# Output projection of a hybrid mLSTM and sparse-attention block: weight quarters through GpSimd's queue, T4 summed early in B22's place, four joins by copies and accumulating DMAs

## The chip, the core and the metric

The kernel runs on one core of a Trainium2 chip. A core has five engines with an instruction queue each: TensorE (PE, matrix products, with PEld for its weight loads), VectorE (DVE), ScalarE (ACT), GpSimd (POOL) and SyncE (SP). An engine runs its own queue in order, and waits on semaphores of the others. DMA transfers are issued from the queues of SP, ACT and POOL; only those issued by POOL may accumulate into what they write. Products land in PSUM, which has eight banks of 128 x 512 float32; everything else lies in SBUF. The metric is the device time of one execution in microseconds (us).

## What is computed

The reference is one decoder layer. Its last part is what matters here:

```
ya = sigmoid(p["m_o"]) * mh * silu(p["m_z"])          # 512 x 1024, branch A
yb = yn * silu(p["n_z"])                              # 512 x 512,  branch B
merged = (sigmoid(p["g_a"]) * (ya @ w_branch_a)
          + sigmoid(p["g_b"]) * (yb @ w_branch_b))    # 512 x 1024
x = x + merged @ w_out                                # 1024 x 1024 weight
return _rmsnorm(x, final_norm_g)
```

All of it is float32. The kernel gets that accuracy by splitting each operand into a rounded high part and the rest (`split`: ACT writes the high part, DVE the low one) and by three matmuls for each product: high by high, high by low, low by high.

## The kernel before

The change lies in the last 100 us, in the block at lines 1231 to 1422.

**Branch A** comes first: eight jobs, one for each block of 128 output columns, in the order j = 0, 4, 1, 5, 2, 6, 3, 7 (L1275). A job is 24 matmuls into one PSUM bank of the tag `pp`, which has three (`branch`, L1111). Its weights come by SP as a 512 KB tile `wr` (three places) and are split into `wh` and `wl` (four places each); its gate `s` (three places, 256 KB) comes by SP from HBM too. A job's loads and the split of its weights are traced two jobs ahead of its matmuls (`Stream`, L164). After the matmuls DVE forms `s = (s + 1) * ps` (L1121) and adds it to branch B's part (`merge`, L1267), which gives a finished block `merged[j]`; `settle` splits the block of the job before into `meh` and `mel`; and after j = 4, 5, 6 `merged_sums` forms the sums and differences that the next part needs, and splits them into `mSh` and `mSl`.

**The output projection** multiplies the 512 x 1024 matrix `merged` by W_out with seven block products in place of eight (Strassen's method in Winograd's form). Tokens and features of `merged` are halved, and W_out is cut into quarters B11, B12 (first 512 rows; left and right columns), B21, B22. Besides quarters, the products take four sums:

- T3 = B12 + B22, T2 = T3 + B11, T4 = T2 + B21, T1 = B12 + B11.

The products are, in TensorE's order, M11 (by B11), M12 (by B21), M22 (by T4), MS2 (by T2), MS3 (by T3), MS1 (by T1), MS4 (by B22); each is 24 matmuls for each of two token blocks, every one of which reads a 128-row block of merged features. M11 needs the blocks j = 0 to 3, so it ends up waiting for job 7 (j = 3) and M12 for job 8 (j = 7). Every factor is made by `hilo`, which splits two half-quarter tiles of 128 x 1024 with the same four `wh` and `wl` places as the branch weights.

How the factors come in before: SP loads B12 into a tile `T` and B22 into tiles `R`, and POOL adds B22 onto that copy by two accumulating DMAs (`added`, L1287), which gives T3. B11, B12 (a second time) and B21 come into `R` by SP. DVE forms T2 = T3 + B11 (L1302). POOL adds B11 onto the second B12, which gives T1. T4 = B21 + T2 is formed by DVE behind M11 (L1376), in B21's place. So W_out is read 1.25 times.

The results go to `xo`, which starts as the residual x. `aside` copies a PSUM bank by ACT, scaled by 0.5 or -0.5, and POOL adds the copy to `xo` by an accumulating DMA: M11 (L1374), and X after MS2 and MS3. `join` has DVE add a bank to `xo` itself (L1334); `joined` adds to that a square by ACT, for the norm, and DVE's product with the final norm's weight.

What sets the order: the functions are traced in the order of the text, but a planner may move every instruction that isn't held, by its own model of durations. `tc.keep_in_program_order` pins an instruction behind the one traced just before it on its engine. Here TensorE is held from L1312 on, and nothing of DVE, ACT, POOL and SP is, except one table load: `ordered` was cleared earlier. So the order of merges, sums, splits and transfers in the profile is the planner's. A place of a tile with several (`bufs`) is given on when its last reader is done.

Of the kernel before, what the change touches and what calls it, by code (L numbers as in the profile page):

```python
# [11 lines left out]
F32 = mybir.dt.float32  # L12
# [3 lines left out]
OP = mybir.AluOpType  # L16
AX = mybir.AxisListType.X

T = 512
D = 1024  # L20
NT = T // 128
ND = D // 128
# [10 lines left out]
NG, NZ, GA, GB = 6408, 6432, 6944, 7968  # L33
# [29 lines left out]
def build(  # L63
# [4 lines left out]
    nc = tc.nc  # L68
    ordered = {"act", "dve"}

    class Engine:
# [3 lines left out]
        def __getattr__(self, op):  # L75
# [7 lines left out]

            return call

    pe, pool = Engine(nc.tensor, "pe"), nc.gpsimd
    act, dve = Engine(nc.scalar, "act"), Engine(nc.vector, "dve")
    A = act.activation
# [40 lines left out]
    def split(src, hi, lo, eng="a"):  # L129
        if eng == "a":  # L130
            A(hi, src, AF.Copy)
        elif eng == "p":
            pool.tensor_scalar(hi, src, 1.0, 1.0, OP.mult, OP.mult)
        else:
            dve.tensor_copy(hi, src)
        dve.tensor_tensor(lo, src, f(hi), OP.subtract)
# [27 lines left out]
    class Stream:  # L164
# [3 lines left out]
        def add(self, load, gen):  # L168
            self.jobs.append((load, gen))
# [56 lines left out]
    stream = Stream(2)  # L226
# [13 lines left out]
    cs = pers.tile([128, NT, 4], F32, name="cs")  # L240
# [36 lines left out]
    def hilo(qs):  # L277
        out = []
        for q in qs:
            hi = wp.tile([128, 2, 512], F32R, name="wh", tag="wh", bufs=4)  # L280
            lo = wp.tile([128, 2, 512], F32R, name="wl", tag="wl", bufs=4)
            split(q, hi, lo)
            out.append((hi, lo))
        return out

    with tc.tile_pool(name="ph0", bufs=2, side="right") as p0, tc.tile_pool(
        name="small", bufs=1, side="right"
# [10 lines left out]
        for k in (0, 4):  # L298
            ks = slice(k, k + 4)
# [10 lines left out]
        for hf in range(2):  # L310
            ps = PS()
# [67 lines left out]
        for tb in range(NT):  # L379
            ts = slice(tb * 128, (tb + 1) * 128)  # L380
            for hf in range(2):
                ks = slice(hf * 4, hf * 4 + 4)
# [55 lines left out]
        split(b, *parts["S1"])  # L438
        split(d, *parts["S4"])

    def plus(dst, a, b):
        for d, x, y in zip(dst, a, b):
            dve.tensor_tensor(d, x, y, OP.add)
        return dst

    def product(banks, k, ws, start=True, tbs=(0, 1), cs=slice(0, 512)):
        ah, al = parts[k]
        for tb in tbs:
            ts = slice(tb * 128, tb * 128 + 128)
            for c in range(4):  # L450
                wh, wl = (w[:, c % 2, cs] for w in ws[c // 2])
                first, last = start and c == 0, c == 3
                m = lambda l, r, first=False, last=False: pe.matmul(
                    banks[tb][:, cs], l, r, start=first, stop=last, skip_group_check=True
                )
                m(ah[:, c, ts], wh, first)
                m(ah[:, c, ts], wl)
                m(al[:, c, ts], wh, False, last)
# [179 lines left out]
    load = lambda: next(more)  # L638
# [372 lines left out]
    late = deque()  # L1011
# [46 lines left out]
    yah = yap.tile([128, ND, T], F32R, name="yah", tag="yah")  # L1058
    yal = yap.tile([128, ND, T], F32R, name="yal", tag="yal")

    sgp = ctx.enter_context(tc.tile_pool(name="sgp", bufs=3))
# [40 lines left out]
    wov = w_out[0].rearrange("(k p) c -> p k c", p=128)  # L1102
# [3 lines left out]
    def branch(base, j, yh, yl, nk):  # L1106
        def gen(w):
            o = 0 if nk == ND else (j % 2) * 128
            ps = PP()
            yield from passes(  # L1110
                ps, lambda k: w[0][:, k, o : o + 128], lambda k: w[1][:, k, o : o + 128],  # L1111
                lambda k: yh[:, k], lambda k: yl[:, k], nk,
            )
            s = halves.pop((base, j))
            if base == GB:
                if not merged:
                    merged.append(pers.tile([128, ND, T], F32, name="mB", tag="hTh"))
                dve.scalar_tensor_tensor(merged[0][:, j], s, 1.0, ps, OP.add, OP.mult)
            else:
                dve.scalar_tensor_tensor(s, s, 1.0, ps, OP.add, OP.mult)  # L1120
                merge(j, s)  # L1121

        def load():
            halves[base, j] = sgp.tile([128, T], F32, name="s", tag="s")
            nc.sync.dma_start(halves[base, j], gD[base, j])
            if nk == ND:
                return weights(wav[:, :, j * 128 : j * 128 + 128])
            if j % 2 == 0:
                halves["w"] = weights(wbv[:, :, j * 128 : j * 128 + 256])
            return halves["w"]  # L1130

        stream.add(load, gen)
# [10 lines left out]
    for h in range(4):  # L1143
# [11 lines left out]
        for sb in range(NT):  # L1155
            o, n = KOFF[sb], 512 - sb * 128
# [6 lines left out]
        for sb in range(NT):  # L1163
            o, n = KOFF[sb], 512 - sb * 128
# [13 lines left out]
        for tb in range(NT):  # L1178
            po = PT()
            for sb in range(tb + 1):  # L1180
                a = KOFF[sb] + (tb - sb) * 128
# [49 lines left out]
    with tc.tile_pool(name="fin", bufs=1, reuse_waits="tile") as fp:  # L1231
# [10 lines left out]
        def merged_sums(i):  # L1242
            a, b = merged[0][:, i], merged[0][:, i + 4]
            a1, a2, b1, b2 = a[:, :256], a[:, 256:], b[:, :256], b[:, 256:]
            dve.tensor_tensor(b2, a2, b2, OP.subtract)
            dve.tensor_tensor(a2, a1, a2, OP.subtract)
            dve.tensor_tensor(a1, b2, a1, OP.subtract)
            dve.tensor_tensor(b1, a1, b1, OP.add)
            sums_split(i, a, 0)

        def sums_split(i, t, c):
            split(
                t, Sh_[:, i, c : c + 2, :].rearrange("p s t -> p (s t)"),
                Sl_[:, i, c : c + 2, :].rearrange("p s t -> p (s t)"),
            )
# [8 lines left out]

        def merge(j, s):
            m = merged[0][:, j]
            dve.tensor_tensor(m, s, m, OP.add)  # L1267
            waiting.append(j)
            if len(waiting) > 1:
                k = settle()  # L1270
                if k in (4, 5, 6):
                    merged_sums(k - 4)

        tc.keep_in_program_order(act.preload_act_table_set("natural_log_exp_and_others"))
        for j in (0, 4, 1, 5, 2, 6, 3, 7):  # L1275
            branch(GA, j, yah, yal, ND)

        def tiles(tag, bufs):
            return [fp.tile([128, 2, 512], F32, name=tag, tag=tag, bufs=bufs) for _ in range(2)]

        def load(i, j, ts):
            for n, t in enumerate(ts):
                ks = slice(i * 4 + n * 2, i * 4 + n * 2 + 2)
                nc.sync.dma_start(t, wov[:, ks, j * 512 : j * 512 + 512])
            return ts

        def added(ts, more):  # L1287
            for t, m in zip(ts, more):
                pool.dma_start(t, m, accum_op=OP.add)
            return ts  # L1290

        t3 = load(0, 1, tiles("T", 4))
        b22 = load(1, 1, tiles("R", 8))
        added(t3, b22)
        stream.run()
        b11 = load(0, 0, tiles("R", 8))
        stream.run()
        b12 = load(0, 1, tiles("R", 8))
        stream.run()
        b21 = load(1, 0, tiles("R", 8))  # L1300
        stream.run()
        t2 = plus(tiles("T", 4), t3, b11)  # L1302
        stream.run(2)
        t1 = added(b12, b11)
        w1 = hilo(b11)
        stream.run()
        settle()
# [6 lines left out]
        xo = yap.tile([128, NT, D], F32, name="xo", tag="yah")  # L1314
        for tb in range(NT):
            nc.sync.dma_start(xo[:, tb], x[0, tb * 128 : tb * 128 + 128, :])
        late = yap.tile([128, 8, 512], F32, name="late", tag="yal")
# [7 lines left out]

        def aside(banks, n, j, half, scale):
            for i, bank in enumerate(banks):
                t, tb = late[:, n * 2 + i], half * 2 + i
                A(t, bank, AF.Copy, scale=scale)
                pool.dma_start(xo[:, tb, j * 512 : j * 512 + 512], t, accum_op=OP.add)  # L1330

        def join(tb, cs, bank):
            xv = xo[:, tb, cs]
            dve.scalar_tensor_tensor(xv, bank, 0.5, xv, OP.mult, OP.add)  # L1334
            return xv

        def joined(tb, cs, bank, n):
            xv = join(tb, cs, bank)
            A(junk[:, tb * 2 + n % 2, : cs.stop - cs.start], xv, AF.Square, accum_out=fs[:, tb, n : n + 1])
            dve.tensor_tensor(xv, xv, fg[:, cs], OP.mult)  # L1340

# [5 lines left out]

        L, R = slice(0, 512), slice(512, 1024)

        def left(tb, bank):  # L1350
            joined(tb, L, bank, 0)
            part_sum(tb, 1)

# [19 lines left out]
        product(X, "M11", w1)  # L1373
        aside(X, 0, 0, 0, 0.5)  # L1374
        Z = [PP() for _ in range(2)]
        t4 = plus(b21, b21, t2)  # L1376
        w4 = hilo(t4)
        product(Z, "M12", w2)
        merged_sums(3)
        w6 = hilo(t2)  # L1380
        V = [PT() for _ in range(2)]
        product(V, "M22", w4)
        ordered.difference_update(("act", "dve"))
        for i in range(2):
            left(i, Z[i])
        for i in range(4):
            sums_split(i, merged[0][:, i + 4], 2)
        for i in range(2):
            join(2 + i, L, V[i])
        w7 = hilo(t3)  # L1390
        product(X, "MS2", w6, False)
        aside(X, 1, 1, 0, -0.5)
        w5 = hilo(t1)
# [51 lines left out]
```

## Time and profile before

| | us |
|---|---|
| median of three runs | 634.77 (634.74 to 635.29) |
| the profiled execution | 637.34 |
| its span, first to last instruction | 635.3 |
| PE busy in the span | 608.0 (96%) |
| DVE busy | 494.0 (78%) |
| ACT busy | 345.9 (54%) |
| POOL busy | 59.1 (9%) |

The profile shows one execution. The timeline lists instructions by start, duration, engine, line, operation, output and inputs, with the idle time of the engine just before them and what ended it in brackets. Nearly all compute instructions have line 79, that of a helper, so they are told apart by their tiles: `pp<-yah,wh` is branch A, `ps<-wh,meh` is M11, `mel<-mB,meh` is the low part of a finished block. Busy times of matmuls overlap: their starts, 0.23 us apart, are the pace. The table of windows gives busy time (and count) of each engine in a stretch, the granted clock of TensorE as a share of full speed, the busy share of the DMA engines, and GB/s.

### The profile page before, as it was taken

The numbers are of one execution on the slowest core, as the hardware profiler recorded it, in microseconds if no ns is written. First come the engines' busy times: TensorE is split into PE (matmuls) and PEld (weight loads), VectorE is DVE, ScalarE is ACT, GpSimd is POOL, SyncE is SP. The second block draws the span as 40 slices with busy tenths as digits, with TensorE's granted clock in tenths as the row PEclk, the third lists the DMA queues.
The fourth block names the chain that finished last, engine by engine and source line by source line (L and its number), as shares of the span: only waits on it lengthen the run. The fifth ranks groups of instructions, "written<-read, shape, count | busy, mean of one in ns | idle before, by whom it ended". The sixth has DMA issues, their size and how long they took to land.

```text
span 635.3 us, 8633 instructions
## 1 busy us (share of the span) xinstructions
PE 608.0 (96%) x3014; PEld 502.5 (79%) x3014; DVE 494.0 (78%) x962; ACT 345.9 (54%) x650; POOL 59.1 (9%) x124
## 2 busy tenths in 40 slices
PE   5999999999999999999999999999999999987995
PEld 3988878888888877888888788887878788866784
DVE  4799979596685777876868676989898986459966
ACT  5645457554442456665665665666565643125564
POOL 4000000000000001221312130000000000100120
PEclk9999999999999999999999999999999999999898
DMA  7925644502067442131322213513232337993324
GB/s 240 336 92 165 214 134 122 173 5 83 18 176 197 107 127 83 51 84 50 84 57 77 84 39 97 146 36 99 67 100 67 100 116 200 297 249 105 111 50 150
DMA packets 83643, 76.02 MB, mean 120 GB/s; under 512 B 4960, under 2 KB 64516, under 8 KB 83600
## 3 DMA queue, kind: packets, MB, share of 16 engines
q1 hardware_dynamic: 82016, 71.53, 37.5%
q0 software_dynamic: 1440, 3.67, 3.3%
q8 instruction: 24, 0.39, 0.3%
q10 hardware_dynamic: 144, 0.26, 0.1%
q14 instruction: 19, 0.16, 0.1%
HBM read 62.35 MB, written 8.39 MB: 111 GB/s over the span
## 4 chain that ended last, share of the span: by engine, by line
PE 67%; DVE 16%; DMA 5%; ACT 5%; issue 4%; POOL 1%; SPq 1%; POOLq 0%; ACTq 0%; DVEq 0%
PE pp L79 38%; PE ps L79 16%; PE pt L79 10%; PE po L79 3%; DVE u L79 3%; DVE wl L79 2%; ACT wh L79 2%; DMA T<-R 1%; DMA R<-w_out 1%; DVE mB L79 1%; DMA wr<-w_branch_a 1%; DVE Dm L79 1%; DMA xt<-x 1%; DVE Sl L79 1%; DVE Th L79 1%
## 5 line engine op out<-in xcount | busy, mean ns | idle before, releaser
L79 PE MATMUL pp<-hTh,wh 128*128 128x512 f32 (+1 forms) x360 | 142.6, 396 | 0.0
L79 PE MATMUL pp<-hTl,wh 128*128 128x512 f32 (+1 forms) x360 | 140.0, 389 | 0.0
L79 PE MATMUL pp<-hTh,wl 128*128 128x512 f32 (+1 forms) x360 | 139.8, 388 | 0.0
L79 ACT ACTIVATE wh<-wr 128x1024 fp32r<-128x1024 f32 x56 | 59.0, 1058 | 59.2 <-PE pp L79 43.9
L79 DVE TENSOR_TENSOR wl<-wr,wh 128x1024 fp32r<-128x1024 f32 x56 | 68.2, 1219 | 17.0 <-ACT wh L79 16.9
L79 PEld LDWEIGHTS pp<-hTh,wl 128*128 128x128 f32 x360 | 67.7, 188 | 13.1
L79 PEld LDWEIGHTS pp<-hTh,wh 128*128 128x128 f32 x360 | 67.8, 188 | 10.6
L79 PEld LDWEIGHTS pp<-hTl,wh 128*128 128x128 f32 x360 | 67.9, 189 | 9.9
L959 POOL TENSOR_SCALAR P<-P,st 128x128 f32<-128x128 f32 (+1 forms) x64 | 34.6, 560 | 160.9 <-DVE st L79 69.0
L79 DVE TENSOR_TENSOR wl<-R,wh 128x1024 fp32r<-128x1024 f32 x28 | 33.9, 1221 | 12.8 <-ACT wh L79 12.7
L79 DVE TENSOR_TENSOR wl<-T,wh 128x1024 fp32r<-128x1024 f32 x28 | 33.8, 1222 | 10.4 <-ACT wh L79 10.4
L79 ACT ACTIVATE P<-P,st 128x128 f32<-128x128 f32 (+3 forms) x64 | 35.5, 555 | 11.2 <-DVE st L79 10.7
L79 ACT ACTIVATE pth<-pt 128x512 fp32r<-128x512 f32 (+1 forms) x64 | 26.9, 434 | 25.9 <-PE pt L79 14.6
L79 DVE TENSOR_TENSOR ptl<-pt,pth 128x512 fp32r<-128x512 f32 (+1 forms) x64 | 29.9, 485 | 14.2 <-ACT pth L79 13.7
L79 DVE CUSTOM_DVE_ANT_0 P<-ps,cst 128x128 f32<-128x128 f32 (+3 forms) x64 | 30.5, 487 | 12.7 <-PE ps L79 12.5
L79 ACT ACTIVATE wh<-R 128x1024 fp32r<-128x1024 f32 x28 | 29.1, 1054 | 16.3 <-PE pt L79 7.1
L79 DVE SCALAR_TENSOR_TENSOR u<-pp,prm,u 128x511 f32<-128x511 f32 (+2 forms) x48 | 35.7, 744 | 0.2
L79 ACT ACTIVATE wh<-T 128x1024 fp32r<-128x1024 f32 x28 | 29.1, 1055 | 12.1 <-PE ps L79 5.6
L79 PE MATMUL ps<-k,Th 128*128 128x256 f32 (+2 forms) x112 | 29.1, 341 | 1.4 <-PE pp L79 0.8
L79 PE MATMUL pt<-cst,P 128*128 128x128 f32 x160 | 28.4, 277 | 0.9 <-DVE ptl L79 0.8
L79 PEld LDWEIGHTS pt<-cst,P 128*128 128x128 f32 x160 | 19.7, 140 | 10.9 <-DVE ptl L79 5.8
L79 PE MATMUL pp<-yah,wh 128*128 128x512 f32 x64 | 25.0, 391 | 2.1 <-ACT wh L79 2.1
(350 smaller groups left out, 1392.6 us busy)
## 6 DMA issues: line engine op xcount, KB each, us to landing
wr<-w_in SPq DMA_DIRECT2D x44, 512.0 KB, 4.0
R<-w_in SPq DMA_DIRECT2D x24, 512.0 KB, 4.6
gD<-sg SPq DMA_DIRECT2D x16, 256.0 KB, 2.0
s<-gD SPq DMA_DIRECT2D x16, 256.0 KB, 5.8
wr<-w_branch_a SPq DMA_DIRECT2D x8, 512.0 KB, 4.1
R<-w_out SPq DMA_DIRECT2D x8, 512.0 KB, 9.5
vD<-cq SPq DMA_DIRECT2D x8, 256.0 KB, 3.7
wr<-vD SPq DMA_DIRECT2D x4, 512.0 KB, 4.1
```

Source lines behind the costliest of these rows:

```text
L79: ins = fn(*args, **kw)
L959: pool.tensor_scalar(pj, pj, st[:, 2, j : j + 1], 1.0, OP.mult, OP.mult)
```

## The change

All four quarters of W_out are loaded by POOL's queue, held there ahead of the first branch A job, each once. T3 becomes a sum by DVE behind job 3, T2 one behind job 4, T4 one behind job 5, written into B22's place; B22 is loaded a second time by SP, behind the second product, for MS4. T1 is still made by POOL, now behind T2. The instructions of `branch` and `merge`, and the three sums, are held in program order on DVE. M12's and M22's two banks each are no longer joined by DVE: `aside` copies them by ACT into places of the tag `s` and POOL adds them to `xo`; `left` of the first two token blocks then starts from `xo`. The split of T3 (`w7`) is traced ahead of it.

```diff
+    keep = tc.keep_in_program_order
...
-    def plus(dst, a, b):
+    def plus(dst, a, b, held=lambda ins: ins):
         for d, x, y in zip(dst, a, b):
-            dve.tensor_tensor(d, x, y, OP.add)
+            held(dve.tensor_tensor(d, x, y, OP.add))
...
-                dve.scalar_tensor_tensor(s, s, 1.0, ps, OP.add, OP.mult)
+                keep(dve.scalar_tensor_tensor(s, s, 1.0, ps, OP.add, OP.mult))
                 merge(j, s)
...
-            dve.tensor_tensor(m, s, m, OP.add)
+            keep(dve.tensor_tensor(m, s, m, OP.add))
...
-        for j in (0, 4, 1, 5, 2, 6, 3, 7):
-            branch(GA, j, yah, yal, ND)
-
...
-        def load(i, j, ts):
+        def load(i, j, ts, queue=pool):
             for n, t in enumerate(ts):
                 ks = slice(i * 4 + n * 2, i * 4 + n * 2 + 2)
-                nc.sync.dma_start(t, wov[:, ks, j * 512 : j * 512 + 512])
+                keep(queue.dma_start(t, wov[:, ks, j * 512 : j * 512 + 512]))
...
-        t3 = load(0, 1, tiles("T", 4))
-        b22 = load(1, 1, tiles("R", 8))
-        added(t3, b22)
+        b12, b22, b11, b21 = (load(i, j, tiles("R", 8)) for i, j in ((0, 1), (1, 1), (0, 0), (1, 0)))
+        for j in (0, 4, 1, 5, 2, 6, 3, 7):
+            branch(GA, j, yah, yal, ND)
+
+        stream.run(3)
+        t3 = plus(tiles("T", 4), b12, b22, keep)
         stream.run()
-        b11 = load(0, 0, tiles("R", 8))
+        t2 = plus(tiles("T", 4), t3, b11, keep)
+        t1 = added(b12, b11)
         stream.run()
-        b12 = load(0, 1, tiles("R", 8))
+        t4 = plus(b22, t2, b21, keep)
         stream.run()
-        b21 = load(1, 0, tiles("R", 8))
-        stream.run()
-        t2 = plus(tiles("T", 4), t3, b11)
-        stream.run(2)
-        t1 = added(b12, b11)
         w1 = hilo(b11)
...
             for i, bank in enumerate(banks):
-                t, tb = late[:, n * 2 + i], half * 2 + i
+                t = sgp.tile([128, T], F32, name="s", tag="s") if n is None else late[:, n * 2 + i]
+                tb = half * 2 + i
...
-            xv = join(tb, cs, bank)
+            xv = xo[:, tb, cs] if bank is None else join(tb, cs, bank)
...
-        def left(tb, bank):
+        def left(tb, bank=None):
...
         Z = [PP() for _ in range(2)]
-        t4 = plus(b21, b21, t2)
         w4 = hilo(t4)
         product(Z, "M12", w2)
+        b22 = load(1, 1, tiles("R", 8), nc.sync)
         merged_sums(3)
         w6 = hilo(t2)
+        aside(Z, None, 0, 0, 0.5)
         V = [PT() for _ in range(2)]
         product(V, "M22", w4)
         ordered.difference_update(("act", "dve"))
-        for i in range(2):
-            left(i, Z[i])
         for i in range(4):
             sums_split(i, merged[0][:, i + 4], 2)
+        aside(V, None, 0, 1, 0.5)
+        w7 = hilo(t3)
         for i in range(2):
-            join(2 + i, L, V[i])
-        w7 = hilo(t3)
+            left(i)
```

## The prediction

> **What bounds the kernel now.** I read the page first: TensorE is busy for 96% of the span, so a gain must come from gaps or a low clock of TensorE, or from the tail behind its last matmul. Its waits from the start of branch A on name all the gaps there are:
>
> ```profile
> PE ps L79 <- ACT meh L79: 3.2, 1, 3.2
> PE pp L79 <- ACT wh L79: 2.1, 1, 2.1
> PE pp L79 <- DVE wl L79: 0.5, 1, 0.5
> ```
>
> The timeline of TensorE gives their places, and the table of windows the clock:
>
> ```profile
> 535.54 0.39 PE L79 MATMUL pp<-yah,wh 128*128 128x512 f32 x1
> 567.96 0.39 PE L79 MATMUL pp<-yah,wl 128*128 128x512 f32 x1
> 570.41 0.50 PE L79 MATMUL pp<-yah,wh 128*128 128x512 f32 x1 [2.07 <-ACT wh L79]
> 572.00 0.39 PE L79 MATMUL pp<-yah,wh 128*128 128x512 f32 x1
> 584.04 0.39 PE L79 MATMUL ps<-wh,mel 128*128 128x512 f32 x1
> 587.61 0.80 PE L79 MATMUL ps<-wh,meh 128*128 128x512 f32 x1 [3.18 <-ACT meh L79]
> 594.22 0.40 PE L79 MATMUL pp<-wh,meh 128*128 128x512 f32 x1
> 627.12 0.28 PE L79 MATMUL pp<-wh,mSl 128*128 128x256 f32 x1
> 585.00:588.00 3.00, 0.39 (x1) 0.39 (x2) 3.00 (x6) 1.91 (x3) 0.00 (x0) 0.86 0.96 362
> 588.00:594.00 6.00, 6.00 (x15) 4.26 (x15) 5.97 (x9) 2.58 (x4) 0.87 (x1) 0.50 0.45 183
> ```
>
> The 144 matmuls of jobs 1 to 6 start from 535.54 to 567.96: 0.2267 us each, 5.44 a job. Against that pace three things are lost. (a) Job 7: from 567.96 to 572.00 lie four steps, 4.04 us for 0.91: **3.13**. (b) M11's tenth matmul, the first that reads block j = 3: 3.57 for 0.23: **3.34**. (c) The 15 matmuls behind it ran at clock 0.50: 594.22 - 587.61 = 6.61 for 3.40: **3.21**. Together **9.68 us**. From 594.22 to the last matmul nothing is lost.
>
> Where do (a) and (b) come from? The timelines of DVE, SP and POOL, read backwards, meet in one wait:
>
> ```profile
> 541.18 0.69 DVE L79 SCALAR_TENSOR_TENSOR s<-s,pp 128x512 f32<-128x512 f32 x1 [3.35 <-PE pp L79]
> 543.65 0.69 DVE L79 TENSOR_TENSOR mel<-mB,meh 128x512 fp32r<-128x512 f32 x1
> 552.57 1.23 DVE L79 TENSOR_TENSOR T<-T,R 128x1024 f32<-128x1024 f32 x1 [8.23 <-DMA T<-R]
> 553.71 0.68 DVE L79 SCALAR_TENSOR_TENSOR s<-s,pp 128x512 f32<-128x512 f32 x1
> 587.95 0.69 DVE L79 TENSOR_TENSOR mel<-mB,meh 128x512 fp32r<-128x512 f32 x1
> 534.65 1.23 SPq L1284 DMA_DIRECT2D R<-w_out  x2
> 542.62 0.34 SPq L1125 DMA_DIRECT2D s<-gD  x1
> 556.15 0.34 SPq L1125 DMA_DIRECT2D s<-gD  x1
> 558.49 0.53 SPq L143 DMA_DIRECT2D wr<-w_branch_a  x1
> 543.88 1.08 POOL L1289 DMA_DIRECT2D T<-R  x1 [16.69 <-DVE wl L79]
> 569.30 1.06 ACT L79 ACTIVATE wh<-wr 128x1024 fp32r<-128x1024 f32 x1 [7.80 <-DMA wr<-w_branch_a]
> ```
>
> DVE's queue has T2 ahead of job 2's merge. T2 waits 8.23 us for T3, which goes from HBM to `R` (from 534.65) and then through an accumulating DMA (from 543.88). Job 2 was done at 535.54 + 2 x 5.44 = 546.4, but its merge begins at 553.71. SP's next gate load waits for that merge (556.15), and job 7's weights stand behind it: issued at 558.49, split at 569.30. That is (a). DVE, late by then, is busy without a gap to the end of M11, and block 3 is ready only with 587.95. That is (b), and (c) follows (b).
>
> **The change part by part.** *Loads and T3.* The copy of B12 (1 MB) and T3's accumulating DMA go; DVE gets T3: two sums of 128x1024 at 1.23 us, behind job 3. T2 can't block job 2 or 3 any more, as the holds put it behind job 4. SP loses ten issues between its gate loads, and job 7's weights wait only for the merge of job 2 or so, some 7 us earlier. I count (a) as gone.
>
> *Do the quarters land in time?* No row shows a plain load by POOL. The nearest rows:
>
> ```profile
> R<-w_out SPq DMA_DIRECT2D x8, 512.0 KB, 9.5
> T<-R POOLq DMA_DIRECT2D x2, 512.0 KB, 9.5
> s<-gD SPq DMA_DIRECT2D x7, 256.0 KB, 8.8
> 540.00:545.00 5.00, 5.00 (x24) 4.14 (x23) 3.12 (x4) 1.70 (x2) 1.08 (x1) 1.00 1.04 384
> 550.00:555.00 5.00, 5.00 (x23) 4.14 (x23) 2.43 (x3) 0.00 (x0) 0.42 (x1) 1.00 0.93 205
> 592.54 0.87 POOL L1330 DMA_DIRECT2D xo<-late  x1 [34.89 <-ACT late L79]
> 618.74 0.87 POOL L1330 DMA_DIRECT2D xo<-late  x1 [2.13 <-ACT late L79]
> ...
> wr<-w_branch_a SPq DMA_DIRECT2D x8, 512.0 KB, 4.1
> ```
>
> Eight issues of 0.87 us are 7 us of POOL. If they start where SP's did (534.65), 4.2 MB and 1.8 MB of gates and weights beside them need 16 to 29 us at 384 to 205 GB/s: all there by 550 to 564, and B12 with B22, the first half, by 543 to 550. T3 stands behind job 3 (551.9) and its sums, at about 556, T2 at about 561, T4 at about 569. At the worst pace a row allows, that of the accumulating pair (9.5 us for two half quarters), they land at 544, 554, 563 and 573; that end is the first rival. I take the upper ends of the plain rates, which are loads from the same tensor: no wait.
>
> The issues kept to 0.87 us where DVE was busy for 5.97 of 6.00 us (588 to 594), so DVE did not hold them up. The Trainium skill, "SBUF — State Buffer", section "SBUF: two separate sides", speaks against the move: while DVE runs an operation that takes the port it shares with GpSimd, GpSimd can't write the descriptors of its DMAs, and loads from SP or ACT don't suffer this. By that, were each of the eight issues held by one sum of 1.23 us, the last quarter would come 10 us later, at up to 574, T4 would wait 5 us, and the time would be the first rival's; the two rows show no hold.
>
> *T4 moved.* Two sums of 1.22 leave the stretch behind M11 and enter branch A, ahead of job 6's merge. Is DVE still in time for block 3? One window and one group carry the sum:
>
> ```profile
> 540.98:588.64 47.66, 41.89 (x180) 33.38 (x178) 31.91 (x49) 15.85 (x21) 3.70 (x4) 0.98 0.76 219
> L79 DVE TENSOR_TENSOR mSl<-mB,mSh 128x512 fp32r<-128x512 f32 x8 | 5.5, 685 | 0.2 <-ACT mSh L79 0.2
> ```
>
> From the end of job 1 to the last split of block 3 DVE worked 31.91 us. T3 and T4 add 4 x 1.22 = 4.9, so 36.8. Without (a), M11's tenth matmul is due at 535.54 + 8 x 5.44 + 9 x 0.227 = 581.1, 40.1 us behind job 1's end. Before job 3 ends DVE has little to do: jobs 1 and 2 bring a merge, a weight split and a block split each (1.4 + 1.2 + 0.7), so it idles 10.9 - 6.6 = 4.3. 36.8 + 4.3 - 40.1 = 1.0 late, if everything that was ahead of block 3 stays ahead; three second-half splits (2.06) and one of M12's weight splits (1.22) needn't be, which makes it 2.3 early. So (b) shrinks to 0 to 1.0; with the order left to the planner I take **0.8**. The clock held in (a), whose longest gap was 2.1, and fell with 3.2, so (c) goes too.
>
> The Trainium skill, "TensorE: Matmul & The Clock Gate", section "Part 1: The HAM clock gate (the "warmup" mystery)", has the clock fall to half after an idle window of about 3.4 us and recover after as much busy time. By that (c) would be 3.4 / 2 = 1.7 us, an estimate, and the sum 1.5 less; the trace shows 6.6 us at half clock, so the measured 3.21 stands.
>
> *Joins.* These rows price them:
>
> ```profile
> 598.35 0.68 DVE L79 SCALAR_TENSOR_TENSOR xo<-pp,xo 128x512 f32<-128x512 f32 x1
> 591.67 0.58 ACT L79 ACTIVATE late<-ps 128x512 f32<-128x512 f32 x1
> DMA to landing us min/median/max: 3.3/3.3/3.4
> 588.64:608.00 19.36, 19.36 (x75) 15.72 (x75) 18.79 (x26) 10.25 (x15) 1.74 (x2) 0.86 0.27 70
> ```
>
> DVE loses 4 x 0.69 = 2.8 us, and T4's 2.4, of a stretch where it was busy 18.79 of 19.36; ACT gains 4 x 0.58 of 9 us free; POOL gains 4 x 0.87. DVE needs the relief now, since TensorE no longer stops for it: the splits of T2 must be there 14.3 us behind block 3 (15 matmuls and two products). The new wait is that of `left`: its square on ACT waits for an accumulating DMA that lands 0.6 + 0.9 + 3.3 = 4.8 us behind M12, and splits may be queued behind it. M22 alone takes 5.44, so I count nothing; bounds -0.4 to +1.5, where 1.5 is a square placed too early by the planner. B22's second load has the product phase to itself and 20 us until MS4: nothing. The tail, 635.3 - 627.1 = 8.2 us from the last matmul, is unchanged.
>
> *Sum.* -3.13 - 3.34 - 3.21 + 0.8 = **-8.9**. The profiled execution goes from 637.3 (2.0 around its span) to 628.4; the median of the runs shown is 2.6 below that execution, and the same gain takes it from 634.77 to **625.9**.
>
> **The rivals.** *First: the stall in front of block 3 stays.* With quarters at the pace of the accumulating pair, T2 waits about 2 us at 561 and T4 about 2 at 571; or DVE's sums hold up POOL's eight issues by 1.23 us each, 10 us in all, and T4 waits 5; or the planner puts more in front of block 3 than I count. Then DVE is 3 us late, TensorE waits about as long as now, and the clock falls again: only (a) is gained, 634.8 - 3.1 = **631.6**. For it: DVE's budget closes to 1 us. Against: the plain rates, and issues of 0.87 us beside a busy DVE.
>
> *Second: slower.* By the holds, job n's merge is pinned behind the instruction traced before it, the low split of job n + 2's weights. A gate load waits for the merge three jobs back. If the planner puts jobs 7's and 8's weights behind those gate loads on SP, there is a loop: merge, gate and weight issue (0.7), landing (4.1 as the page's median for these weights, 8.8 as gates took in the crowd), splits by ACT and DVE (1.1 + 1.2), the next held merge (1.4): 8.5 to 13.2 us a turn against 5.44 of a job. Two turns at the long end cost 15.5 us and a fall of the clock 3.2, against 9.7 gained: +9, **643.8**. It decides from turns of about 8.7 us, where two cost 6.5 and the clock 3.2. Against: SP has fewer issues, so these weights stand earlier in line than now.
>
> *Third: no change.* POOL's loads find their places taken until late (R's memory is that of the stage before), so T3's wait only moves from T2 to T3 itself, with everything held behind it: within 1 us of 634.8.
>
> **How the numbers follow.** The forecast, 623.9 to 628.4 (from 9.68 and 1.2 of relief in the tail down to 2.5 us less than the sum), 0.68; the first rival, 628.4 to 633.5, 0.16 (0.08 late quarters, 0.02 held issues, 0.06 the planner); no change 0.05; slower 0.11. What a measurement can tell from no change is about 0.2%, 1.3 us. Faster 0.83, same 0.06, slower 0.11. The range reaches from 623.9 to 632.0, over the first rival's price.
>
> **What would show it.** Right: no wait of TensorE on `wh<-wr`; branch A in 43.5 us; M11's wait under 1.5 and clock 1.0 behind it; T3, T2 and T4 on DVE without a wait on a DMA; 8 us of tail. Wrong: a DVE wait on `R<-w_out`; weights of job 7 or 8 issued later than 560; ACT's square waiting on an accumulating DMA with a split behind it and TensorE behind that.

## The result, and the profile after

| | before | after |
|---|---|---|
| median (range) of four runs each | 634.75 (633.47 to 635.29) | 628.94 (628.35 to 629.45) |
| the profiled execution | 637.34 | 628.35 |
| its span | 635.3 | 626.6 |
| TensorE: first matmul of branch A to the last of all | 91.6 | 82.9 |
| last matmul to the end of the span | 8.2 | 9.0 |

The ratio is 0.9911 with a 95% interval of 0.9894 to 0.9928: 5.8 us faster. Between the two profiled executions it is 9.0 us, which is the -8.9 of the sum; by medians only two thirds of that came. Both numbers have to be explained. One execution of the unchanged kernel, in the first experiment, took 2235.32 us and stands in no ratio.

TensorE's waits after, in the part from branch A on, are down to one line:

```profile
PE ps L79 <- ACT late L79: 0.7, 1, 0.7
```

Its timeline: first matmul of branch A, the one place with a wait, and the last matmul.

```profile
534.74 0.39 PE L79 MATMUL pp<-yah,wh 128*128 128x512 f32 x1
...
599.80 0.39 PE L79 MATMUL ps<-wh,mSl 128*128 128x512 f32 x1
600.93 0.50 PE L79 MATMUL ps<-wh,mSh 128*128 128x512 f32 x1 [0.75 <-ACT late L79]
601.27 0.39 PE L79 MATMUL ps<-wl,mSh 128*128 128x512 f32 x1
...
617.60 0.28 PE L79 MATMUL pp<-wh,mSl 128*128 128x256 f32 x1
```

The waits for job 7's weights and for block 3 are gone. What is new is a step of 1.13 us at the start of MS3, and one of 0.34 behind it: 1.0 us more than at pace. (A product is 24 matmuls in all, 12 for each token block, and not 24 for each: M11, M12, M22 and MS2 start 5.44 us apart, at 578.26, 583.70, 589.14 and 594.58.) The other engines of branch A, from the timelines of POOL, SP and DVE:

```profile
526.33 3.15 POOL L1282 DMA_DIRECT2D R<-w_out  x4
532.81 2.88 POOL L1282 DMA_DIRECT2D R<-w_out  x4 [3.33 <-DVE mB L79]
...
537.07 0.38 SPq L144 DMA_DIRECT2D wr<-w_branch_a  x1
...
542.96 1.28 SPq L144 DMA_DIRECT2D wr<-w_branch_a  x1
...
546.53 0.69 DVE L79 SCALAR_TENSOR_TENSOR s<-s,pp 128x512 f32<-128x512 f32 x1 [3.00 <-DMA s<-gD]
...
552.97 1.22 DVE L79 TENSOR_TENSOR T<-R 128x1024 f32<-128x1024 f32 x1
...
556.44 1.22 DVE L79 TENSOR_TENSOR T<-T,R 128x1024 f32<-128x1024 f32 x1
...
567.07 2.35 DVE L79 TENSOR_TENSOR R<-T,R 128x1024 f32<-128x1024 f32 x2
...
577.76 0.68 DVE L79 TENSOR_TENSOR mel<-mB,meh 128x512 fp32r<-128x512 f32 x1
```

The quarters take POOL 3.15 and 2.88 us to issue, from 526.33 on, the weights of jobs 7 and 8 at 537.07 and 542.96 (before, job 7's at 558.49). T3, T2 and T4 wait for no DMA. The one wait on a DMA, 3.00 us for a gate, costs TensorE nothing. Block 3's low split begins at 577.76, 2.5 us ahead of the first matmul that reads block 3 (534.74 + 8 x 5.44 + 9 x 0.227 = 580.3). The table of windows, before and then after, with the DMA share and GB/s at the end of each row:

```profile
535.00:570.00 35.00, 33.34 (x148) 27.27 (x146) 16.14 (x23) 6.90 (x9) 3.70 (x4) 1.00 1.00 279
...
535.00:570.00 35.00, 35.00 (x156) 29.00 (x155) 28.02 (x39) 12.52 (x16) 2.51 (x3) 1.00 0.70 201
```

In these 35 us of branch A before had DVE busy for 16.1 us, the DMA engines for 1.00 of the time, and 279 GB/s. After, DVE has done 28.0 us of work by 570, and the DMA engines stood still for 30% of the time.

### The profile page after: what moved, and what is told of

Read it like the earlier page. It is cut to its first block, busy times and chain, and to the rows that moved or that the text cites. A ratio compares the mean times of both kernels' runs of the same rounds, so it can differ in the third digit from the quotient of the medians.

```text
span 626.6 us, 8638 instructions
## 1 busy us (share of the span) xinstructions
PE 603.6 (96%) x3014; PEld 500.3 (80%) x3014; DVE 492.5 (79%) x960; ACT 347.9 (56%) x654; POOL 67.3 (11%) x134
## 4 chain that ended last, share of the span: by engine, by line
PE 72%; DVE 14%; ACT 6%; issue 4%; DMA 1%; POOL 1%; SPq 0%; ACTq 0%; POOLq 0%; DVEq 0%
PE pp L79 44%; PE ps L79 17%; PE pt L79 9%; PE po L79 3%; DVE u L79 3%; DVE wl L79 2%; ACT wh L79 2%; DVE Dm L79 1%; DMA xt<-x 1%; DVE P L79 1%; ACT P L79 1%; DVE Sl L79 1%; DVE Th L79 1%; DVE xo L79 1%; DVE qkl L79 1%
## 5 line engine op out<-in xcount | busy, mean ns | idle before, releaser
L79 ACT ACTIVATE wh<-R 128x1024 fp32r<-128x1024 f32 x28 | 29.3, 1059 | 18.4 <-PE pt L79 7.1
L79 PE MATMUL pp<-yah,wl 128*128 128x512 f32 x64 | 24.9, 389 | 0.0
```

The costliest lines, as they stand in the source:

```text
L79: ins = fn(*args, **kw)
```

## The experiments

Ratios are to runs of the kernel before that were taken together with the variant, on the same chip.

### How much of the loss is there every time? The kernel before, three more profiles

All three are the unchanged kernel; the first was also timed over ten executions.

> The kernel before once more. Theory V (what a cold stretch of TensorE costs differs from execution to execution): the spans of its executions differ by 1 to 3 us, the granted clock goes down where the span goes up, and the profiled one shows the same two waits of about 3 us each, but a stretch at half clock behind M11's wait that is shorter than the 6.6 us of the first profile, or none. Rival (the profile itself slows the kernel before by 2.6 us): all executions have spans within 0.5 us of each other and clocks within 0.001, and the stretch is 6.6 us again.

> The kernel before once more, unchanged: what differs between its executions. Theory W (the stretch at half clock behind the wait for block 3 is long or short, 6.5 or 3.5 us, from one execution to the next, worth 1.5 us): some profile of this kernel has a stretch under 5 us, and the span is about 1.5 us shorter with it. Rival U (the stretch is always about 6.5 us; the scatter of 3 us between executions comes from the stages ahead of branch A): the stretch is again 6 to 6.6 us, and the distance from the first matmul of branch A to the last stays 91.5 us, while the first moves by 1 us or more.

> The same kernel before, a second look. Theory W: a stretch under 5 us in one of the two looks. Rival U: 6 to 6.6 us in both, 91.5 us from first to last matmul, and the difference ahead of branch A.

The timed one: 635.46, ratio 1.0002 [0.9989, 1.0014]. The single times of the kernel before that enter the ratios run from 632.64 to 637.25, so the profiled execution of 637.34, on which the sum was made, lies above all of them. The three profiles have TensorE's waits in the same two places, but the half clock falls elsewhere and lasts differently. Windows of the third profile (e12; the column before the last two is the granted clock), at job 7 and at M11's tenth matmul:

```profile
571.00:577.00 6.00, 5.96 (x20) 4.29 (x20) 5.86 (x11) 3.78 (x6) 0.00 (x0) 0.75 0.01 3
...
585.00:590.00 5.00, 2.87 (x8) 1.66 (x7) 5.00 (x8) 2.56 (x4) 0.00 (x0) 0.77 0.85 342
590.00:594.00 4.00, 4.00 (x17) 3.24 (x16) 3.97 (x5) 2.55 (x4) 0.87 (x1) 0.87 0.51 207
```

and of the fourth (e13):

```profile
566.00:571.00 5.00, 2.77 (x10) 1.48 (x8) 1.20 (x2) 1.58 (x2) 0.00 (x0) 0.86 0.84 236
571.00:577.00 6.00, 5.96 (x16) 4.67 (x16) 5.88 (x11) 4.50 (x6) 0.00 (x0) 0.55 0.03 6
...
585.00:590.00 5.00, 3.98 (x17) 2.67 (x16) 4.97 (x8) 1.80 (x3) 0.00 (x0) 1.00 0.94 311
```

A clock of 0.75 over 6 us is 2 x 0.25 x 6 = 3.0 us at half clock. So read, e12 has 3.4 us of it behind job 7's wait (0.4 lie ahead of 571) and 3.3 behind block 3's; e13 has 6.8 us behind job 7's and none behind block 3's, whose wait has shrunk to 0.7 (DVE, it seems, catches up while TensorE is slow). Before, by the two rows of the prediction, has 2 x (0.14 x 3 + 0.50 x 6) = 6.8 us, all of it behind block 3, and so has the timed one. The stretches come as about 3.4 or 6.8 us, in one place, in the other, or in both.

The Trainium skill, "TensorE: Matmul & The Clock Gate", section "Part 1: The HAM clock gate (the "warmup" mystery)", says that the window in which the clock is decided runs freely, so that the same kernel may differ from run to run. These profiles agree, with stretches of one and of two of its 3.4 us; and where that page of the Trainium skill wants an idle window of about 3.4 us, a wait of 2.1 us for job 7 sufficed in e12 and did not in before.

From the first matmul of branch A to the last, the four profiles of before take 91.6, 91.5, 90.1 and 89.2 us; with 81.9 at pace they lose 9.7, 9.6, 8.2 and 7.3. Theory V was right in the scatter (spans of 632.0 to 635.1 us) and wrong in the stretch, which was 6.8 us again in the timed one. Of the answers on e12 and e13 both were partly right: the stretch varies (theory W), and the rival's 91.5 held in neither; but e13 kept 6.8 us in all.

### Only the blocking sum: the kernel before with merges and T2 held

```diff
-                dve.scalar_tensor_tensor(s, s, 1.0, ps, OP.add, OP.mult)
+                keep(dve.scalar_tensor_tensor(s, s, 1.0, ps, OP.add, OP.mult))
...
-            dve.tensor_tensor(m, s, m, OP.add)
+            keep(dve.tensor_tensor(m, s, m, OP.add))
...
-        t2 = plus(tiles("T", 4), t3, b11)
+        t2 = plus(tiles("T", 4), t3, b11, keep)
```

> The kernel before with nothing changed but the holds on DVE: the merges and T2 (behind job 4) stay in program order; loads, T3's accumulating DMA, T4 behind M11 and the joins stay as before. Theory H (the planner's place for T2 ahead of job 2's merge caused the waits): no wait of TensorE on branch A's weights, M11's wait under 1.5 us, time 627 to 630. Rival L (the loads on SP's queue and the crowd of transfers caused them): weights of job 7 still late, time within 1.5 us of the kernel before.

633.41, ratio 0.9967 [0.9954, 0.998]: 1.6 to 2 us, not 6 to 9. T2 runs at 555.02 without a wait and blocks no merge, so the wait that I had named as the cause was gone. Theory H falls: TensorE's wait for job 7's weights went down to 0.2 us, but another wait for block 3 took the old one's place, behind late weights, as rival L has it. Timelines of SP, ACT, DVE and PE:

```profile
549.10 0.56 SPq L144 DMA_DIRECT2D wr<-w_branch_a  x1
...
565.96 1.06 ACT L79 ACTIVATE wh<-wr 128x1024 fp32r<-128x1024 f32 x1 [11.58 <-DMA wr<-w_branch_a]
...
567.05 1.23 DVE L79 TENSOR_TENSOR wl<-wr,wh 128x1024 fp32r<-128x1024 f32 x1 [9.08 <-ACT wh L79]
...
585.13 0.50 PE L79 MATMUL ps<-wh,meh 128*128 128x512 f32 x1 [4.00 <-ACT meh L79]
```

Job 7's weights, issued 9 us earlier than before, take 16.9 us to land. DVE's next instruction is their split; it stands for 9.08 us with merges and sums queued behind it, and block 3 is 4.00 us late.

### Only the early loads: the kernel before with all W_out loads ahead of branch A on POOL

```diff
-                nc.sync.dma_start(t, wov[:, ks, j * 512 : j * 512 + 512])
+                tc.keep_in_program_order(pool.dma_start(t, wov[:, ks, j * 512 : j * 512 + 512]))
...
-        b22 = load(1, 1, tiles("R", 8))
+        b22, b11, b12, b21 = (load(i, j, tiles("R", 8)) for i, j in ((1, 1), (0, 0), (0, 1), (1, 0)))
+        for j in (0, 4, 1, 5, 2, 6, 3, 7):
+            branch(GA, j, yah, yal, ND)
         added(t3, b22)
```

T3 is still B12 plus B22 by two accumulating DMAs, and B12 is loaded twice.

> The kernel before, with all its loads of W_out (five quarters, B12 twice) held on POOL's queue ahead of branch A; T3 is still B12 plus B22 by POOL's accumulating DMAs, and T2, T4, T1 and the joins are as before. Theory E (the gain comes from having the quarters early, off SP's queue between gates and weights; who makes T3 doesn't matter): T3 lands by about 555, T2 waits under 1 us, job 7's weights are issued before 550, the waits of 2.1 and 3.2 us go, clock 1.00: 628 to 630. Rival S (the accumulating transfer is what blocks, wherever the loads stand): POOL's accumulating DMAs wait behind the loads, DVE waits 2 us or more for T, and either (a) or (b) stays: 631 to 635.

633.71, ratio 0.9974 [0.9958, 0.9989]. What theory E asks for happens (no wait of DVE for T, the weights issued before 550, TensorE's wait for them gone), but not its time, so it falls; rival S's time came, though not by its wait. Again it is the weights. SP, ACT and PE:

```profile
537.10 0.38 SPq L143 DMA_DIRECT2D wr<-w_branch_a  x1
...
543.00 0.38 SPq L143 DMA_DIRECT2D wr<-w_branch_a  x1
...
556.95 1.06 ACT L79 ACTIVATE wh<-wr 128x1024 fp32r<-128x1024 f32 x1 [5.37 <-DMA wr<-w_branch_a]
...
565.99 1.06 ACT L79 ACTIVATE wh<-wr 128x1024 fp32r<-128x1024 f32 x1 [7.46 <-DMA wr<-w_branch_a]
...
584.50 0.50 PE L79 MATMUL ps<-wh,meh 128*128 128x512 f32 x1 [4.00 <-ACT meh L79]
```

They are issued at the same moments as after the change (537.07 and 542.96) and land 20 and 23 us later; after, the second one took 8.3. So an early issue of the weights is not enough. (The quarters themselves are not quite as early here: of their ten loads one is issued at 526.38 and the rest between 532.78 and 541.39, where after issues four of eight from 526.33 on.) The DMA view of 535 to 570 (queue: packets, MB, share of the time of 16 engines; q0 is POOL's queue, q1 that of SP) and its windows show why:

```profile
q0 software_dynamic: 1872, 6.82, 67.8%
q1 hardware_dynamic: 2876, 2.35, 22.1%
...
T<-R POOLq DMA_DIRECT2D x2, 512.0 KB, 14.4
R<-R POOLq DMA_DIRECT2D x2, 512.0 KB, 13.4
```

```profile
555.00:560.00 5.00, 5.00 (x24) 4.14 (x23) 1.96 (x3) 1.58 (x2) 0.00 (x0) 1.00 1.08 236
560.00:565.00 5.00, 5.00 (x24) 4.14 (x23) 2.74 (x3) 0.00 (x0) 0.00 (x0) 1.00 1.03 262
```

The DMA engines are full up to 565, at 236 to 262 GB/s, where a row of the prediction has 384: the two accumulating pairs take 13 to 14 us each to land and fill the engines with few bytes. In the profile of before the same view has POOL's queue with nothing but the two pairs:

```profile
q1 hardware_dynamic: 5561, 7.66, 65.7%
q0 software_dynamic: 576, 2.10, 33.6%
```

That is 2.10 MB in 33.6% of 35 us: 5.6 us of all 16 engines per MB. SP's plain transfers have 7.66 MB in 65.7%: 3.0 us per MB. At these rates one pair (1.05 MB) and the second B12 (1.05 MB), which the change removes, are an estimated 5.9 + 3.1 = 9 of 35 us.

The Trainium skill, "DMA: Bandwidth & Descriptors", section "🔬 Queues, rings and completion order", says that an engine goes round its queues a whole packet at a time. This profile fits it: POOL's packets have 6.82 MB / 1872 = 3.6 KB and SP's 0.8 KB, so a full POOL queue would leave SP's weights a small share. No run varies the packets alone, so that this is the reason is not shown.

### Only the sum: the changed kernel with its loads back on SP among the jobs

```diff
-        def load(i, j, ts, queue=pool):
+        def load(i, j, ts, queue=nc.sync):
...
-                keep(queue.dma_start(t, wov[:, ks, j * 512 : j * 512 + 512]))
+                queue.dma_start(t, wov[:, ks, j * 512 : j * 512 + 512])
...
-        stream.run(3)
+        b12, b22 = (load(i, j, tiles("R", 8)) for i, j in ((0, 1), (1, 1)))
+        stream.run()
+        b11 = load(0, 0, tiles("R", 8))
+        stream.run(2)
+        b21 = load(1, 0, tiles("R", 8))
```

> The changed kernel with the quarters issued by SP among the jobs, unheld and traced as in the kernel before (first half ahead of job 2's gate, the rest between later gates and weights); T3, T2, T4 as DVE's sums, the joins as changed. Rival S (T3 as a plain sum suffices, the place of the loads doesn't matter): no wait in branch A over 0.5 us, only the 0.75 us at MS3: 628 to 630. Theory E (early loads are what counts): job 7's weights are issued later than 548 or T3's or T2's sums wait over 2 us on R, so TensorE waits 2 us or more for a weight split or for block 3: 631 to 635.

627.26, ratio 0.9876 [0.9842, 0.9909], the lowest time of all kernels here. Rival S is right in its mechanism, theory E falls; the time is below the 628 to 630 of rival S, where the wait at MS3 is gone too and the tail is 8.2. TensorE runs from 535.24 to 617.05 (81.8 us) without one late step, although the weights of jobs 7 and 8 are issued later than theory E allows. SP and ACT:

```profile
542.71 0.43 SPq L1282 DMA_DIRECT2D R<-w_out  x1
547.76 0.34 SPq L1126 DMA_DIRECT2D s<-gD  x1
548.15 0.43 SPq L1282 DMA_DIRECT2D R<-w_out  x1
548.67 1.04 SPq L144 DMA_DIRECT2D wr<-w_branch_a  x2
...
554.90 1.06 ACT L79 ACTIVATE wh<-wr 128x1024 fp32r<-128x1024 f32 x1 [2.86 <-DMA wr<-w_branch_a]
...
566.92 6.53 SPq L1282 DMA_DIRECT2D R<-w_out  x2
```

Issued at 548.67, much as in the run with holds alone (549.10), the weights land in 6 us in place of 17. Of what differs ahead of these weights, the transfers are the accumulating pair of T3 and the second B12. Set beside each other, from the windows of 535 to 570:

| kernel | DMA engines busy | GB/s | DVE busy, us | wait for block 3, us |
|---|---|---|---|---|
| before | 1.00 | 279 | 16.1 | 3.2 |
| before, holds alone | 0.93 | 273 | 18.4 | 4.0 |
| before, early loads alone | 0.90 | 262 | 19.2 | 4.0 |
| sum alone, loads among jobs | 0.83 | 243 | 27.5 | none |
| after, quarters by SP (below) | 0.80 | 237 | 27.5 | none |
| after | 0.70 | 201 | 28.0 | none |

The pair and the second load of B12 were not taken away one without the other; which of the two does more is open.

### Parts that do nothing: holds, POOL's queue, T4's place

Each is the changed kernel with one part undone: no holds on DVE; the eight loads by SP in the same place; T4's sums behind M11 again.

```diff
-                keep(dve.scalar_tensor_tensor(s, s, 1.0, ps, OP.add, OP.mult))
+                dve.scalar_tensor_tensor(s, s, 1.0, ps, OP.add, OP.mult)
```

> The changed kernel without the holds on DVE's merges and sums; the planner then puts T3 ahead of job 2's merge. Theory P (what counts is that the quarters are there early and T3 is no chain of two transfers): T3 finds B12 and B22 landed, no wait on a DMA over 2 us, time 628 to 630. Rival H (the order on DVE was the cause): DVE waits 5 us or more in front of a merge, M11's wait of about 3 us and the half clock are back, 632 to 635.

```diff
-        def load(i, j, ts, queue=pool):
+        def load(i, j, ts, queue=nc.sync):
```

> The changed kernel with the four quarters issued by SP, in the same place, in place of POOL; SP then issues the weights of jobs 7 and 8 only behind the gate of job 5. Theory Q (the queue matters, since weights that stand behind 4 MB of quarters on one queue come 10 us and more after their issue, as in the run with the holds alone): job 7's weights are late, DVE waits for their split, a wait of TensorE is back, time 630 to 635. Rival (once T3 is a sum and the order is held, SP has room): 628 to 630, no wait of TensorE in branch A.

```diff
-        t4 = plus(b22, t2, b21, keep)
         w1 = hilo(b11)
...
         Z = [PP() for _ in range(2)]
+        t4 = plus(b22, t2, b21, keep)
```

> The changed kernel with T4 formed behind M11 again, all else as changed. Theory D (DVE is some 2 us early for block 3 and TensorE never waits for it, so the place of T4 is worth nothing): within 0.6 us of the changed kernel. Rival (T4's 2.4 us behind M11 make the splits of T4 and T2 late): a wait of TensorE of 1 to 2 us at M22 or MS2, 630 to 631.

628.44 (0.9902 [0.9882, 0.9922]), 628.76 (0.9906 [0.9887, 0.9925]) and 628.87 (0.9906 [0.9883, 0.9928]): all three as fast as the change (theory Q and rival H fall, P and D stand), none with a wait in branch A, each with the 0.8 to 0.9 us at MS3. Without holds the planner puts T3 at once behind job 1, at 543.30, and finds both quarters there. By SP the eight issues take the queue 6.5 us (534.16 to 540.69) and put the weights of jobs 7 and 8 at 548.94, which is early enough. Each part was undone alone, with the others kept: no run leaves out the holds and the early loads together.

### The joins and B22's second load

Three variants of the changed kernel: the four joins by DVE again; B22's second load issued by ACT behind the split of T2, which is behind the residual's crowd; and this with, also, the second pair of X copies and B22's split pinned ahead of the squares on ACT.

```diff
-        aside(Z, None, 0, 0, 0.5)
-        aside(V, None, 0, 1, 0.5)
...
+        for i in range(2):
+            left(i, Z[i])
...
-            left(i)
+            join(2 + i, L, V[i])
```

> The changed kernel with the four joins by DVE again, everything else as changed. Theory S (the joins by copy and accumulating DMA cost 1 us, because ACT's first square waits 5 us for a landing): TensorE's wait at the first matmul of MS3 goes, the tail behind the last matmul is back at 8.2 us from 9.0, time 1 to 1.8 us under the changed kernel. Rival (DVE needs the relief): a wait of TensorE on splits of T2 or T3 takes its place, time the same or more.

```diff
-        b22 = load(1, 1, tiles("R", 8), nc.sync)
         merged_sums(3)
         w6 = hilo(t2)
+        b22 = load(1, 1, tiles("R", 8), nc.scalar)
```

> The changed kernel with B22's second load issued by ACT behind T2's split, some 10 us later, in place of SP right behind the residual's loads. Theory S with the crowd as its cause (M11's accumulating DMAs take 8 us to land among 3.6 MB of loads, so the next ones and the square are late): M11's accumulating DMAs land in 3 to 4 us, no wait at MS3, time 0.7 to 1.3 us under the changed kernel. Rival (the square is late for its own chain of copy, issue and landing): the wait at MS3 stays at about 1 us, same time.

```diff
+        aside(X, 2, 1, 1, -0.5, keep)
+        ordered.add("act")
+        w3 = hilo(b22)
+        ordered.remove("act")
...
-        aside(X, 2, 1, 1, -0.5)
```

> The kernel with B22's later load, and besides it the copies of X behind MS3 and the split of B22 ahead of the squares on ACT. Theory E (the end is set by a chain from the second copy of X: issue, landing, join of block 3 and 8.7 us of DVE work): the copy starts 0.5 to 1.5 us sooner behind MS3 and the tail behind the last matmul shrinks from 9.0 to between 8.0 and 8.5 us, time 0.4 to 1.0 us under e3_b22_later (627.0 to 627.5). Rival (the end hangs on the last matmul alone): the tail stays at 9.0, same time as e3_b22_later.

628.32 (0.9887 [0.987, 0.9903]), 627.90 (0.9883 [0.9868, 0.9897]) and 627.66 (0.9886 [0.9866, 0.9905]). By medians that is 0.6 to 1.3 us under the change, by ratios 1.5 to 1.8. In none of the three does the profile list the wait at MS3, and from the first matmul to the last they take 82.6, 82.3 and 82.3 us in place of 82.9. Not all of it is gone: with the joins back, small steps in MS2 cost 0.7 us, and with B22 later the step at MS3 is still 0.5 us, 0.4 too much with the one behind it. The timelines of after tell why both edits help, SP, POOL and ACT in turn:

```profile
578.65 1.90 SPq L1313 DMA_DIRECT2D xo<-x  x4
580.73 0.94 SPq L1282 DMA_DIRECT2D R<-w_out  x2
...
585.75 0.85 POOL L1328 DMA_DIRECT2D xo<-late  x1 [0.18 <-issue]
592.86 0.85 POOL L1328 DMA_DIRECT2D xo<-s  x1 [6.26 <-DMA xo<-late]
...
596.20 0.63 ACT L79 ACTIVATE junk<-xo 128x512 f32<-128x512 f32 x1 [5.25 <-issue]
...
600.29 0.59 ACT L79 ACTIVATE late<-ps 128x512 f32<-128x512 f32 x1
```

B22 (1 MB) is issued right behind the residual (2 MB). M11's copies are added to `xo` in that crowd and land after 7.9 us (median of the DMA view), M12's follow them onto the same columns, and the square of `left` waits for those. It stands at the head of ACT's queue for 5.25 us. So the copy that takes MS2's result out of the bank that MS3 needs (600.29) starts 3.2 us behind the start of the last MS2 matmul into it (597.08), where the sum-alone kernel has 0.5. With B22 behind the crowd (the second variant), or ahead of it as the planner has it in the sum-alone kernel (566.92 there), M11's copies land in 5.1 us (3 to 4 were expected), and in the latter ACT waits 2.55. So the whole wait needs both edits at once: joins through POOL, and B22 in the residual's crowd. The four kernels in which the profile does not list it have ratios of 0.9876 to 0.9887, the four others with T3 as a sum 0.9902 to 0.9911: 1.0 to 2.2 us, though single pairs of intervals overlap; of TensorE's time from branch A on it is 0.2 to 1.2 us.

## Why the prediction was right, and where not

**Losses.** The three terms were right in place and, for that execution, in size: after, none is left, and the clock is 1.00 throughout. That the profiled executions differ by 9.0, against 8.9 forecast, is partly luck. The 9.7 went in full, where 8.9 was expected; 1.0 was lost at MS3 and 0.8 in the tail; and the other 1.0 lies elsewhere: branch A starts 0.8 us earlier (534.74 against 535.54, where the four profiles of before alone scatter from 534.46 to 535.66), and 0.2 lies outside the span.

**The step that failed is the last one of the sum, "the same gain takes it from 634.77 to 625.9".** 9.68 us is the loss of an execution 2.6 us above the median; the four profiles show 7.3 to 9.7 for the same program. (c) is not a fixed 3.2, and (b) is smaller where the clock falls at (a). Working back from the medians: a gain of 5.8, with 1.0 lost at MS3 and 0.8 in the tail, puts the loss removed in a typical run at about 7.6, an estimate. The four profiles agree with it: they lose 8.7 in the mean, and their executions lie 1.2 us above 634.75 in the mean. With 2.1 less to gain, 1.8 lost elsewhere and 0.8 better at block 3, the forecast was about 3 us too low.

**The residual at block 3**, counted as 0.8, was 0: DVE began the low split of block 3 2.5 us early, slightly past the favourable end of "1.0 late to 2.3 early".

**Joins and B22's second load**, counted as nothing, cost 1.0 in the trace. The mechanism stood among the bounds (+1.5, "a square placed too early by the planner") and the signs of being wrong. What I left out is that B22's load does not have "the product phase to itself": the residual is loaded at the same moment.

**The tail** was taken as unchanged and grew from 8.2 to 9.0. The joins are not its cause: with them back it is 8.9. Half of the growth lies in the work of DVE and ACT, up to the start of ACT's last scaling, which begins 3.8 us behind the last matmul's start before and 4.1 after. This half goes with the place of the last copy on ACT, 9.26 us ahead of the last matmul in before and in the sum-alone kernel (tail 8.2 in both) and 8.8 after. The other half lies in that scaling and the transfer of the result behind it: from its start to the end it is 4.5 us before and 4.85 after, but 4.5 with the quarters by SP, whose copy stands at 8.86, and 4.84 with the copy pinned early at 10.9. So the place of the copy does not explain it. Pinning the copy brought the tail to 8.4, and nothing that these runs can tell in time (ratios 0.9883 without, 0.9886 with it). The second half stays open.

**The cause.** The chain back to T2's wait for T3 was read correctly, but I gave the cure to the wrong parts: "T2 can't block job 2 or 3 any more, as the holds put it behind job 4". Taking away that block alone gives 1.6 us, since a crowd of transfers stands behind it: the weights of jobs 7 and 8 are still late in landing, and DVE waits for those. I had counted (a) gone because the weights would be *issued* some 7 us earlier (it was 21); the early-loads run shows the same issue time with a landing of 20 us. What cures it is T3 as a DVE sum, with the accumulating pair and the second B12 out of branch A's transfers; which of these two does more was not tested. The holds, POOL's queue, T4's place and the early loads change nothing measurable when one of them is taken back from the changed kernel.

**The rivals.** By its time alone, 628.94, the result lies 0.5 us above the forecast's own 623.9 to 628.4 and in the first rival's 628.4 to 633.5. But what the first rival says, a stall in front of block 3, did not come: TensorE waits nowhere in branch A or M11. None of the three came about. The first one's fear, quarters at the pace of the accumulating pair (9.5 us), was right in the pace: they took 8.8 us. But POOL issues them from 526.33 on, not from SP's 534.65 as I assumed, and without the holds T3 found the first half there at 543.30. DVE did not hold up POOL's issues: eight took 6.0 us, where by that rival they would have come 10 us late.

## What to carry to other kernels

When an engine waits for a transfer, ask what its removal leaves next in line: here most transfers of the stage were late; another order or an earlier issue alone gave 1.6 to 2 us, and only less DMA work gave the rest. Price an accumulating DMA by the time it takes of the DMA engines, and so from the loads beside it, not by its own landing. And if the profiled execution lies above the median, part of the loss read from it is that execution's own: scale the gain, or take a second profile.

## What was unexpected of the hardware

Accumulating transfers between two places in SBUF took 5.6 us of all 16 DMA engines per MB, plain loads from HBM 3.0 (before, 535 to 570; 5.0 and 2.9 with the holds alone); no run parts the accumulating from the place. A 256 KB one onto `xo` landed in 3.4 us with little beside it (before) and in 7.9 beside 3 MB of loads (after). A 512 KB weight load issued at the same time landed after 8.3 us (after) or after 23 us (early loads alone); what POOL's queue holds beside it differs. The half clock came in stretches of 3.4 or 6.8 us, behind waits of 2.1 to 4.0 us, and not always behind the same one.
